# FFN duos with the last up product collected onto a difference in its PSUM bank, the plain up pair at the duo's end, and x reloaded in eight parts

## The chip, the cores and the metric

The kernel runs on one core of a Trainium2 chip. The metric is the device time of the whole program in microseconds, the median of its runs. Times in the profile are microseconds from the start of the profiled execution, unless marked ns. Engines: PE is TensorE, DVE VectorE, ACT ScalarE, POOL GpSimd, SP the engine that issues most DMAs here.

## The reference

A decoder trunk for 256 tokens, d_model 2048, d_ff 5632, all in float32: a layer with gated linear attention (GLA) and an FFN, then shared keys and values, then a layer with differential attention and an FFN. The change is in the two FFNs:

```python
def swiglu(h, w_gate_up, w_down):
    gate, up = jnp.split(h @ w_gate_up, 2, axis=-1)
    return (jax.nn.silu(gate) * up) @ w_down
...
f = swiglu(rmsnorm(x, pre_ffn_g[i]), ffn_w_gate_up[i], ffn_w_down[i])
x = x + rmsnorm(f, post_ffn_g[i])
```

The rows of `rmsnorm` are scaled late: a factor `rs[b]` per token of the 128-token half b (b = 0, 1) is applied to the products.

## The kernel before, in words

**Split products.** Every float32 operand is split into a `hi` and a `lo` part, and each product is three matmuls (`triple`, L482 to 488: hi x hi, hi x lo, lo x hi). A weight sub-tile of 128 x 1024 is loaded by SP into a ring of 5 tiles `raw` (L263), cast to `hi` by ACT (L298) and its rest `lo` = raw - hi made by DVE (L301), in a ring of 9 (NRING). A matmul has 512 columns, so a sub-tile serves two k-blocks (j = 0, 1) of 128 rows, with 512 output columns. The sub-tiles follow one order written by `weight_stream`, the same in which `take` asks for them.

**An FFN.** There are 11 chunks c of 512 gate columns; gate chunk c and up chunk 11 + c make one gated chunk `sg` (silu(gate) x up, 2 halves of 128 tokens). PE transposes it (`split_T`, L655), ACT and DVE split it into `f_ffn_gT` (L657, L658), and the down product (`down_act`, `mm_act`, L411 to 413) uses it. `ffn_steps` mixes up chunks with down steps of earlier groups, FF_GROUPS = ((0, 1), (2, 3), (4, 5), (6, 7), (8,), (9, 10)). Down sums of a group start from the sum so far, copied by ACT into PSUM (L464), and are brought out by ACT (L1261).

**A duo.** Chunk 0 is computed plainly. For c = 1 to 10, `gated_duo` computes gate and up chunk together; I call it duo c. The k dimension has 8 steps s of two k-blocks. At fast steps (s = 0, 2, 3, 4, 5, 6; for c = 1: 0, 2, 4, 6) the 2 x 2 block product (two token halves and two k-blocks by two column chunks) takes 7 products instead of 8, with sums of weights made by DVE (L333, four adds of 512 a step) and sums of h made once (`f_ffn_fast`, `f_ffn_rest`). Each fast step takes four converted sub-steps: "a" (wide, banks 0 and 1), "b" (wide, banks 6 and 2), "c" (wide, banks 5 and 3) and "d" (512 wide, bank 4): 7 x 3 = 21 matmuls. At plain steps (s = 1 and 7; for c = 1: 1, 3, 5, 7) gate goes straight to banks 1 and 3 (token halves 0 and 1) and up to banks 2 and 7, 12 matmuls each. `duo_apart` (the version with bank 7 of its own) runs this in the order of s.

**The end of a duo.** After the last fast step `early` brings out ACT's copy sg0 = bank 0, then on DVE v = bank 5 - sg0, sg1 = bank 6 - v, y = bank 4 - sg1, v = bank 4 + v. After the gate's step 7 `late` adds banks 1 and 3 to sg0 and sg1 and applies Silu. After the up part's step 7 it adds bank 2 to v and bank 7 to y (L1186), and `gated` multiplies each into sg (L1190). `gate_T`, with the transposes, follows some ticks later (`defer`; a tick is one product group). EARLY_BEHIND and LATE_BEHIND hold `early` and `late` behind the conversions of so many of the next sub-steps (`behind`).

**Order.** A framework lays the program out per engine by its own timeline and picks buffers of the pools; each engine then runs its instructions in that order. PSUM has six banks of pool `acc` and two of pool `tp`; in a duo, banks 0 to 5 come from `acc`, 6 and 7 from `tp`. x lies in DRAM meanwhile; at the start of the last down step `reload` (L1463) brings it back in two DMAs of 1 MB for the residual sum at the FFN's end (`after` in FFN 0, then the norm `h_kv` for the next stage, L705).

Of the kernel before, what the change touches and what calls it, by code (L numbers as in the profile page):

```python
# [82 lines left out]
def weight_stream():  # L83

    out = []

    def chunk(name, n, ns=8, s0=0):
        out.extend((name, (n, s0 + s), "plain") for s in range(ns))

    def block(name, n):  # L90
        out.extend((name, (n, s), "plain") for s in range(2))

    def duo(c1, c2, fast):
        for s in range(8):
            if s in fast:
# [24 lines left out]
    def middle_duo(name, fast):  # L120
        chunk(name, 0)
        duo((name, 1), (name, 2), fast)
        chunk(name, 3)

    middle_duo("gla_w_out", FAST_OUT)
    ffn(0)
    chunk("w_v", 0)
    chunk("w_v", 3)
    duo(("w_v", 1), ("w_v", 2), FAST_V)
    for name in ("w_k", "diff_w_q"):  # L130
        for n in range(KT):
            block(name, n)
    middle_duo("diff_w_out", FAST_OUT)
    ffn(1)
    return out

# [52 lines left out]
class Trunk:  # L189
# [289 lines left out]
            for u in range(n, len(order)):  # L479
                run(u, b)  # L480

    def triple(self, ps, a, w, j, first, last):  # L482
        nc = self.nc
        ah, al = a
        wh, wl = (t[:, j * C : (j + 1) * C] for t in w)
        nc.tensor.matmul(ps, ah, wh, start=first, stop=False)  # L486
        nc.tensor.matmul(ps, ah, wl, start=False, stop=False)  # L487
        nc.tensor.matmul(ps, al, wh, start=False, stop=last)  # L488

    def duo_act(self, aT, forms, fast, c1, c2, early, late):  # L490

# [688 lines left out]
    def gated_duo(self, hT, forms, w, c, rs, new_sg):  # L1180

        nc = self.nc
        made = []

        def op(out, in0, in1, how):
            nc.vector.tensor_tensor(out=out, in0=in0, in1=in1, op=how)  # L1186

        def gated(b, up):
            sg = made[0]
            nc.vector.scalar_tensor_tensor(  # L1190
                out=sg[:, b, :], in0=up, scalar=rs[b], in1=sg[:, b, :], op0=ALU.mult, op1=ALU.mult
            )

        def early(ps):
            made.extend((new_sg(), self.scratch(), self.scratch()))
            sg, v, y = made
            nc.scalar.copy(sg[:, 0, :], ps[0])
            op(v, ps[5], sg[:, 0, :], ALU.subtract)
            op(sg[:, 1, :], ps[6], v, ALU.subtract)
            op(y, ps[4], sg[:, 1, :], ALU.subtract)  # L1200
            op(v, ps[4], v, ALU.add)

        def late(bank, ps):
            sg, v, y = made
# [9 lines left out]
        self.duo_apart(hT, forms, ffn_pairs(c), ((w, c), (w, 11 + c)), early, late)  # L1214
        return made[0]

    def ffn(self, fp, hT, rs, gi, wgu, wd, post, after, name, reload, side=None):
# [55 lines left out]
        for n, (kind, which, *chunks) in enumerate(plan):  # L1273
            if kind == "up":
                sg = self.gated_duo(hT, forms, wgu, which, rs, new_sg) if which else gated_first()
                follow = plan[n + 1]
                wait = 4
                if follow[0] == "down" and which not in follow[1]:
                    wait = 2 * len(down_order(*follow[1:])) + 1
                self.defer(wait, lambda sg=sg, c=which: gate_T(sg, c))  # L1280
                continue
            chunks, skew = chunks[0], 0
            if not f:
                f.append(self.whole(5, [P, 2, D], name))
# [168 lines left out]
    def run(self):  # L1453
# [6 lines left out]
        def reload(src, name):  # L1460
            self.x = self.whole(4, [P, 2, D], name)
            for b in range(2):
                nc.sync.dma_start(self.x[:, b, :], src[b])  # L1463

        with tc.tile_pool(name="gla", bufs=1) as gp:
            oT = self.gla(gp, hT, rs)
            rs = []
# [16 lines left out]
        with tc.tile_pool(name="ffn0", bufs=1) as fp:  # L1484
# [9 lines left out]
            self.ffn(fp, hT, rs, 1, "w_gu0", "w_d0", t["post_ffn_g"][0:1], after, "f_ffn0", lambda: reload(x_mix0, "x_ffn0"), self.setup_diff)  # L1494

        hq = Split([None, None])

# [52 lines left out]
        with tc.tile_pool(name="ffn1", bufs=1) as fp:  # L1550

            def store(b, xs):
                for c, xc in enumerate(xs):
                    nc.sync.dma_start(t["out"][b * P : (b + 1) * P, c * C : (c + 1) * C], xc)

            self.ffn(fp, hT, rs, 0, "w_gu1", "w_d1", t["post_ffn_g"][1:2], store, "f_ffn1", lambda: reload(x_mix1, "x_ffn1"))


@with_exitstack
# [89 lines left out]
```

## Time and profile before

| | us |
|---|---|
| three runs | 2168.75, 2168.73, 2167.71; median 2168.73 |
| profiled execution | 2168.14, of which the span from first to last instruction is 2166.4 |
| mean granted clock of TensorE | 0.999 |

The span holds the GLA layer up to about 400 us, FFN 0 to about 1080, values, keys, queries, attention and its output to about 1480, and FFN 1 to the end. In the rows of the profile stand: the start and duration of an instruction (or of a run of equal ones, "x3" with the time of all), its engine, line and operation, out<-in by the program's names, and in square brackets how long the engine had been idle and who released it. A group's row has the line, shapes, count, busy time and the mean of one in ns, then the idle time ahead of them. A window's row has each engine's busy time in that stretch. A row of waits has the total, the number and the longest. In the profile `hs` is a scratch tile (v or y here).

### The profile page before, as it was taken

What the parts mean: (1) busy time and instruction counts of PE and PEld (TensorE: products, weight loads), DVE (VectorE), ACT (ScalarE), POOL (GpSimd) and SP (SyncE); (2) the same over time, 40 slices, a digit from 0 to 9 for tenths busy, and PEclk for the clock granted to TensorE, in tenths of its full rate; (3) what the DMA queues carried; (4) which work ended last, traced back from release to release, by engine and by line L of the source; (5) the groups of instructions that cost most, each with busy time, mean ns of one, the idle gap of its engine ahead of it and who ended that gap; (6) DMA issues with size and microseconds to landing.
All of it is one profiled execution on the core that took longest, in us unless ns stands there. A gap on an engine that the chain in (4) does not pass through costs nothing.

```text
span 2166.4 us, 28415 instructions
## 1 busy us (share of the span) xinstructions
PE 2151.2 (99%) x10044; PEld 1787.7 (83%) x10044; DVE 1953.3 (90%) x2686; ACT 1374.2 (63%) x1926; POOL 37.1 (2%) x66
## 2 busy tenths in 40 slices
PE   9999999999999999999999999999999999999998
PEld 8888788888888888888778888888888888888886
DVE  7989988999999999999798567889999999999996
ACT  8756655666666666666776445556656666666664
POOL 1000000000000000000000000000000000000000
PEclk9999999999999999999999999999999999999999
DMA  8546566666565666656767655465665566665664
GB/s 310 166 150 192 174 226 219 219 199 227 173 209 203 211 211 195 223 190 211 254 200 245 185 179 159 155 226 202 225 195 187 177 207 214 212 209 201 203 225 155
DMA packets 123317, 440.10 MB, mean 203 GB/s; under 512 B 13900, under 2 KB 16629, under 8 KB 121381
## 3 DMA queue, kind: packets, MB, share of 16 engines
q1 hardware_dynamic: 121996, 436.44, 60.4%
q10 hardware_dynamic: 1176, 1.84, 0.2%
q8 instruction: 79, 1.29, 0.2%
q14 instruction: 66, 0.53, 0.1%
HBM read 429.82 MB, written 9.97 MB: 203 GB/s over the span
## 4 chain that ended last, share of the span: by engine, by line
PE 93%; DVE 4%; issue 1%; ACT 1%; DMA 1%; SPq 0%; POOL 0%; DVEq 0%; POOLq 0%; ACTq 0%
PE acc L488 12%; PE acc L487 12%; PE acc L486 12%; PE acc L413 11%; PE acc L412 11%; PE acc L411 11%; PE acc L634 8%; PE acc L635 4%; PE tp L487 2%; PE tp L486 2%; PE tp L488 2%; DVE lo L301 2%; PE tp L655 1%; DVE raw L333 1%; DMA raw<-in_w_d_dram 1%
## 5 line engine op out<-in xcount | busy, mean ns | idle before, releaser
L301 DVE TENSOR_TENSOR lo<-raw,hi 128x1024 fp32r<-128x1024 f32 x921 | 1096.2, 1220 | 115.1 <-ACT hi L298 108.8
L298 ACT CAST hi<-raw 128x1024 fp32r<-128x1024 f32 x923 | 943.9, 1051 | 356.5 <-DVE raw L333 91.5
L412 PE MATMUL acc<-lo,f_ffn_gT 128*128 128x512 f32 x704 | 273.5, 389 | 0.1
L411 PE MATMUL acc<-hi,f_ffn_gT 128*128 128x512 f32 x704 | 270.4, 389 | 0.0
L413 PE MATMUL acc<-hi,f_ffn_gT 128*128 128x512 f32 x704 | 269.0, 389 | 0.0
L487 PE MATMUL acc<-lo,h_ffn 128*128 128x512 f32 x612 | 238.7, 390 | 0.0
L488 PE MATMUL acc<-hi,h_ffn 128*128 128x512 f32 x612 | 238.4, 389 | 0.0
L486 PE MATMUL acc<-hi,h_ffn 128*128 128x512 f32 x612 | 227.8, 390 | 0.0
L333 DVE TENSOR_TENSOR raw<-raw 128x512 f32<-128x512 f32 x232 | 159.5, 687 | 3.4
L411 PEld LDWEIGHTS acc<-hi,f_ffn_gT 128*128 128x128 f32 x704 | 132.2, 188 | 28.4 <-issue 0.6
L412 PEld LDWEIGHTS acc<-lo,f_ffn_gT 128*128 128x128 f32 x704 | 132.1, 188 | 27.9 <-DVE lo L301 0.6
L413 PEld LDWEIGHTS acc<-hi,f_ffn_gT 128*128 128x128 f32 x704 | 132.2, 188 | 27.4
L486 PEld LDWEIGHTS acc<-hi,h_ffn 128*128 128x128 f32 x612 | 114.9, 188 | 24.2 <-ACT hi L298 0.4
L488 PEld LDWEIGHTS acc<-hi,h_ffn 128*128 128x128 f32 x612 | 114.9, 188 | 23.5
L487 PEld LDWEIGHTS acc<-lo,h_ffn 128*128 128x128 f32 x612 | 114.9, 188 | 23.5
L298 ACT CAST hi<-sum 128x512 fp32r<-128x512 f32 x72 | 44.8, 622 | 101.1 <-DVE sum L333 101.1
L634 PE MATMUL acc<-h_q,hi 128*128 128x512 f32 x256 | 92.5, 401 | 0.0
L634 PE MATMUL acc<-h_kv,hi 128*128 128x512 f32 x256 | 90.7, 399 | 0.0
L634 PE MATMUL acc<-h_mix,hi 128*128 128x512 f32 x256 | 90.6, 398 | 0.0
L1261 ACT COPY f_ffn<-acc 128x512 f32<-128x512 f32 x80 | 45.8, 586 | 66.4 <-PE acc L413 66.4
L298 ACT CAST f_ffn_rest<-sum 128x512 fp32r<-128x512 f32 x56 | 34.9, 623 | 80.9 <-DVE sum L333 80.9
L333 DVE TENSOR_TENSOR sum<-raw,raw 128x512 f32<-128x512 f32 x116 | 79.4, 685 | 0.0
(415 smaller groups left out, 4128.6 us busy)
## 6 DMA issues: line engine op xcount, KB each, us to landing
raw<-in_w_gu_dram SPq DMA_DIRECT2D x352, 512.0 KB, 4.5
raw<-in_w_d_dram SPq DMA_DIRECT2D x176, 512.0 KB, 4.8
raw<-in_gla_w_r_dram SPq DMA_DIRECT2D x32, 512.0 KB, 4.8
raw<-in_gla_w_v_dram SPq DMA_DIRECT2D x32, 512.0 KB, 4.1
raw<-in_gla_w_out_dram SPq DMA_DIRECT2D x32, 512.0 KB, 4.5
raw<-in_w_v_dram SPq DMA_DIRECT2D x32, 512.0 KB, 4.4
raw<-in_w_k_dram SPq DMA_DIRECT2D x32, 512.0 KB, 4.4
raw<-in_diff_w_q_dram SPq DMA_DIRECT2D x32, 512.0 KB, 3.5
```

Of the source, the lines that this page charges most:

```text
L298: cast = nc.scalar.copy(hi, src)
L301: rest = eng.tensor_tensor(out=lo, in0=src, in1=hi.bitcast(F32), op=ALU.subtract)
L333: return self.nc.vector.tensor_tensor(out=out, in0=in0, in1=in1, op=ALU.add)
L411: nc.tensor.matmul(ps, ah, rh, start=(kt == 0 and not onto), stop=False, skip_group_check=onto)
L412: nc.tensor.matmul(ps, ah, rl, start=False, stop=False, skip_group_check=onto)
L413: nc.tensor.matmul(ps, al, rh, start=False, stop=(kt == 2 * ns - 1), skip_group_check=onto)
L486: nc.tensor.matmul(ps, ah, wh, start=first, stop=False)
L487: nc.tensor.matmul(ps, ah, wl, start=False, stop=False)
L488: nc.tensor.matmul(ps, al, wh, start=False, stop=last)
L634: nc.tensor.matmul(ps, lh, aT.both(kt), start=(kt == 0), stop=False)
L635: nc.tensor.matmul(ps[:, SEQ:], ll, aT.hi(kt), start=False, stop=(kt == KT - 1))
L1261: nc.scalar.copy(fc, ps)
```

## The change

`duo_seeded` takes the place of `duo_apart` in the FFNs (proj_out and values keep `duo_apart`).

- At the plain steps ahead of the last fast step only the gate's sub-tile stays. The up sub-tile of such a step ("kept") moves behind the last fast step, ahead of the gate's step 7; `weight_stream` is changed alike. Its bank 2 part runs at once, its bank 7 part after the gate's step 7.
- `early` has no y: it writes bank 4 - sg1 straight into PSUM bank 7, which is opened after the last fast step. The matmuls of bank 7 then all accumulate onto it (no `start`), and `late` gives bank 7 to `gated` as it is. One DVE add per duo is gone.
- Bank 7 now comes from `acc`, and banks 2 and 6 from `tp`.
- `early` is `urgent` (high priority), EARLY_BEHIND goes from 3 to 1, and chunk 0's `gate_T` waits 1 tick and not 4.
- x is reloaded as 8 DMAs of 256 KB, deferred by 4 + 3n ticks.

```diff
-EARLY_BEHIND, LATE_BEHIND, DOWN_BEHIND, GATE_BEHIND = 3, 3, 0, 0
+RELOAD_BEGIN, RELOAD_EVERY = 4, 3
+EARLY_BEHIND, LATE_BEHIND, DOWN_BEHIND, GATE_BEHIND = 1, 3, 0, 0
...
+    def duo_seeded(self, aT, forms, fast, chunks, early, late):
...
+        def bank_of(bank):
+            if bank not in ps:
+                ps[bank] = self.tp().rearrange("p j t -> p (j t)") if bank in (2, 6) else self.acc()
+                return True
+            return False
+
+        def add(bank, a, wp, j, last, onto=False):
+            first = bank_of(bank)
+            self.triple(ps[bank], a, wp, j, first and not onto, last, onto)
...
+            if s not in fast:
+                wp = self.take(w1, (n1, s))
+                for b, bank in enumerate((1, 3)):
+                    plain(bank, s, b, wp, False)
+                self.free()
+                held.append(s)
+                continue
...
+            if last:
+                bank_of(7)
+                with self.behind(EARLY_BEHIND):
+                    self.urgent(early)(ps)
+        kept = [(s, self.take(w2, (n2, s))) for s in held]
+        for s, wp in kept:
+            plain(2, s, 0, wp, False)
+        wp = self.take(w1, (n1, 7))
+        for b, bank in enumerate((1, 3)):
+            plain(bank, 7, b, wp, True)
+        for s, wp2 in kept:
+            plain(7, s, 1, wp2, False, True)
+            self.free()
+        self.free()
+        wp = self.take(w2, (n2, 7))
+        plain(2, 7, 0, wp, True)
+        plain(7, 7, 1, wp, True, True)
+        self.free()
...
         def early(ps):
-            made.extend((new_sg(), self.scratch(), self.scratch()))
-            sg, v, y = made
+            made.extend((new_sg(), self.scratch()))
+            sg, v = made
...
-            op(y, ps[4], sg[:, 1, :], ALU.subtract)
+            op(ps[7], ps[4], sg[:, 1, :], ALU.subtract)
...
+            elif bank == 2:
+                op(v, ps[bank], v, ALU.add)
+                gated(0, v)
             else:
-                b, part = (0, v) if bank == 2 else (1, y)
-                op(part, ps[bank], part, ALU.add)
-                gated(b, part)
+                gated(1, ps[bank])
...
-                wait = 4
+                wait = 4 if which else 1
...
+        def reload_by_parts(src, name):
+            self.x = x = self.whole(4, [P, 2, D], name)
+            for n in range(8):
+                b, c = n // 4, slice(n % 4 * C, (n % 4 + 1) * C)
+                self.defer(RELOAD_BEGIN + RELOAD_EVERY * n, lambda b=b, c=c: nc.sync.dma_start(x[:, b, c], src[b][:, c]))
```

The order of instructions at three places follows; a number behind a name tells tiles of one kind apart.

ACT at the start of duo 5 of FFN 0, before. `f_ffn0_4438<-acc` are the evacuations of the down step that ran ahead of it, the `hi` are wide casts of weights, and `f_ffn0_rest<-sum` is the narrow cast of a fast step's sub-step "d" (which uses spare room in that tile):

```order
L298 CAST hi_1168_6112<-raw_1144_5988 128x1024
L298 CAST hi_1171_6146<-raw_1150_6012 128x1024
L298 CAST hi_1176_6168<-raw_1153_6021 128x1024
L298 CAST hi_1179_6186<-raw_1159_6049 128x1024
L1261 COPY f_ffn0_4438<-acc_1174_6152 128x512
L1261 COPY f_ffn0_4438<-acc_1175_6153 128x512
L298 CAST f_ffn0_rest_3649<-sum_1181_6202 128x512
L657 CAST f_ffn0_gT4_6243<-tp_1190_6244 128x4x128
L298 CAST hi_1182_6207<-raw_1167_6098 128x1024
```

The same place after:

```order
L306 CAST hi_1164_6104<-raw_1140_5975 128x1024
L306 CAST hi_1167_6138<-raw_1146_5996 128x1024
L306 CAST hi_1172_6160<-raw_1152_6038 128x1024
L306 CAST f_ffn0_rest_3649<-sum_1174_6176 128x512
L306 CAST hi_1175_6181<-raw_1155_6044 128x1024
L1335 COPY f_ffn0_4436<-acc_1170_6144 128x512
L1335 COPY f_ffn0_4436<-acc_1171_6145 128x512
L306 CAST hi_1178_6199<-raw_1152_6038 128x1024
L306 CAST hi_1183_6229<-raw_1163_6090 128x1024
```

The narrow cast of the first fast step, and the wide cast next to it, stood behind the two evacuations and now stand ahead of them.

DVE at the end of duo 10 of FFN 0, before: `acc` and `tp` are PSUM banks, `hs` scratch, `raw_1795` the first down weight, and `sg` the gated chunk:

```order
L301 TENSOR_TENSOR lo_1816_9184<-raw_1795_9098,hi_1815_9183 128x1024
L1186 TENSOR_TENSOR hs_1837_9256<-acc_1767_8967,sg_1836_9255 128x512
L301 TENSOR_TENSOR lo_1819_9196<-raw_1803_9132,hi_1818_9195 128x1024
L1186 TENSOR_TENSOR sg_1836_9255<-tp_1763_8955,hs_1837_9256 128x512
L1186 TENSOR_TENSOR sg_1836_9255<-acc_1758_8932,sg_1836_9255 128x512
L301 TENSOR_TENSOR lo_1822_9205<-raw_1806_9144,hi_1821_9204 128x1024
L1186 TENSOR_TENSOR hs_1838_9257<-acc_1773_8986,sg_1836_9255 128x512
L1186 TENSOR_TENSOR hs_1837_9256<-acc_1773_8986,hs_1837_9256 128x512
L301 TENSOR_TENSOR lo_1825_9217<-raw_1811_9163,hi_1824_9216 128x1024
L301 TENSOR_TENSOR lo_1828_9229<-raw_1814_9175,hi_1827_9228 128x1024
L1186 TENSOR_TENSOR sg_1836_9255<-acc_1768_8971,sg_1836_9255 128x512
L1186 TENSOR_TENSOR hs_1838_9257<-tp_1777_9016,hs_1838_9257 128x512
```

The same place after, where `raw_1790` is the first down weight and `acc_1823` is bank 7:

```order
L1259 TENSOR_TENSOR hs_1825_9220<-acc_1759_8954,sg_1824_9219 128x512
L309 TENSOR_TENSOR lo_1800_9135<-raw_1779_9049,hi_1799_9134 128x1024
L1259 TENSOR_TENSOR sg_1824_9219<-tp_1753_8935,hs_1825_9220 128x512
L309 TENSOR_TENSOR lo_1803_9147<-raw_1782_9061,hi_1802_9146 128x1024
L309 TENSOR_TENSOR lo_1806_9159<-raw_1790_9095,hi_1805_9158 128x1024
L1259 TENSOR_TENSOR acc_1823_9218<-acc_1764_8968,sg_1824_9219 128x512
L1259 TENSOR_TENSOR hs_1825_9220<-acc_1764_8968,hs_1825_9220 128x512
L309 TENSOR_TENSOR lo_1809_9168<-raw_1793_9107,hi_1808_9167 128x1024
L1259 TENSOR_TENSOR sg_1824_9219<-acc_1748_8912,sg_1824_9219 128x512
L1259 TENSOR_TENSOR sg_1824_9219<-acc_1760_8958,sg_1824_9219 128x512
L309 TENSOR_TENSOR lo_1812_9180<-raw_1798_9126,hi_1811_9179 128x1024
L1259 TENSOR_TENSOR hs_1825_9220<-tp_1754_8939,hs_1825_9220 128x512
```

The difference goes into `acc_1823`; the add of the earlier bank 7 (`tp_1777`) into scratch, the last row before, is gone, and the adds of banks 1 and 3 stand next to each other. The first `lo` of a down weight stands ahead of the difference.

SP around the reload of FFN 0, before; `w_gu0` are gate and up weights of duo 10, `w_d0` down weights:

```order
L263 DMA raw_1783_9042<-in_w_gu0_dram 128x1024
L263 DMA raw_1786_9054<-in_w_gu0_dram 128x1024
L1463 DMA x_ffn0_9307<-x_mix0_2816 128x2048 x2
L263 DMA raw_1792_9086<-in_w_gu0_dram 128x1024
L263 DMA raw_1795_9098<-in_w_d0_dram 128x1024
L263 DMA raw_1803_9132<-in_w_d0_dram 128x1024
```

And after:

```order
L271 DMA raw_1773_9017<-in_w_gu0_dram 128x1024
L1543 DMA x_ffn0_9287<-x_mix0_2816 128x512 x3
L271 DMA raw_1779_9049<-in_w_gu0_dram 128x1024
L1543 DMA x_ffn0_9287<-x_mix0_2816 128x512 x2
L271 DMA raw_1782_9061<-in_w_gu0_dram 128x1024
L1543 DMA x_ffn0_9287<-x_mix0_2816 128x512 x3
L271 DMA raw_1790_9095<-in_w_d0_dram 128x1024
L271 DMA raw_1793_9107<-in_w_d0_dram 128x1024
```

The eight parts stand in three clumps between the last two `w_gu0` loads and the first `w_d0` load; of the 2 MB none has moved behind a `w_d0` load.

More of the change, by code (lines that the diff above doesn't have):

```diff
@@ L93, in duo @@
     def duo(c1, c2, fast):
+        apart = c1[0][:4] == "w_gu"
+        kept = [s for s in range(7) if s not in fast] if apart else []
         for s in range(8):
+            if s == 7:
+                out.extend((c2[0], (c2[1], s), "plain") for s in kept)
+            if s in kept:
+                out.append((c1[0], (c1[1], s), "plain"))
+                continue
             if s in fast:
@@ L480, in down_act, with plain @@
                 run(u, b)
-    def triple(self, ps, a, w, j, first, last):
+    def duo_seeded(self, aT, forms, fast, chunks, early, late):
+        ps, held = {}, []
+        (w1, n1), (w2, n2) = chunks
+        def bank_of(bank):
[6 more added lines that the diff above has]
+            self.triple(ps[bank], a, wp, j, first and not onto, last, onto)
+        def plain(bank, s, b, wp, last, onto=False):
+            for j in range(2):
+                add(bank, aT.tokens(2 * s + j, b), wp, j, last and j == 1, onto)
+            if last:
+                with self.behind(LATE_BEHIND):
+                    late(bank, ps)
+            self.tick()
+        for s in range(7):
+            k1, k2 = 2 * s, 2 * s + 1
+            if s not in fast:
[4 more added lines that the diff above has]
+                held.append(s)
+                continue
+            f, last = forms.pairs.index(s), s == fast[-1]
+            plan = {
+                "a": ((0, aT.tokens(k1, 0)), (1, aT.tokens(k2, 0))),
+                "b": ((6, forms.fast(f, 2)), (2, forms.fast(f, 3))),
+                "c": ((5, forms.fast(f, 1)), (3, aT.tokens(k2, 1))),
+                "d": ((4, forms.fast(f, 0)),),
+            }
+            for kind, prods in plan.items():
+                wp = self.take("duo", (*chunks, s), kind)
+                for j, (bank, a) in enumerate(prods):
+                    add(bank, a, wp, j, last and bank in (0, 4, 5, 6))
+                self.free()
+                if kind != "d":
+                    self.tick()
+            if last:
+                bank_of(7)
[14 more added lines that the diff above has]
+        plain(7, 7, 1, wp, True, True)
+        self.free()
@@ L483, in triple @@
+    def triple(self, ps, a, w, j, first, last, onto=False):
         nc = self.nc
@@ L485, in triple @@
         wh, wl = (t[:, j * C : (j + 1) * C] for t in w)
-        nc.tensor.matmul(ps, ah, wh, start=first, stop=False)
-        nc.tensor.matmul(ps, ah, wl, start=False, stop=False)
-        nc.tensor.matmul(ps, al, wh, start=False, stop=last)
+        nc.tensor.matmul(ps, ah, wh, start=first, stop=False, skip_group_check=onto)
+        nc.tensor.matmul(ps, ah, wl, start=False, stop=False, skip_group_check=onto)
+        nc.tensor.matmul(ps, al, wh, start=False, stop=last, skip_group_check=onto)
     def duo_act(self, aT, forms, fast, c1, c2, early, late):
@@ L1199, in early @@
             op(sg[:, 1, :], ps[6], v, ALU.subtract)
[L1200 removed]
+            op(ps[7], ps[4], sg[:, 1, :], ALU.subtract)
             op(v, ps[4], v, ALU.add)
         def late(bank, ps):
[L1204 removed]
+            sg, v = made
             if bank in (1, 3):
@@ L1208, in late @@
                 nc.scalar.activation(sg[:, b, :], sg[:, b, :], AF.Silu, scale=rs[b])
-            else:
-                b, part = (0, v) if bank == 2 else (1, y)
-                op(part, ps[bank], part, ALU.add)
-                gated(b, part)
-        self.duo_apart(hT, forms, ffn_pairs(c), ((w, c), (w, 11 + c)), early, late)
+            elif bank == 2:
+                op(v, ps[bank], v, ALU.add)
+                gated(0, v)
+            else:
+                gated(1, ps[bank])
+        self.duo_seeded(hT, forms, ffn_pairs(c), ((w, c), (w, 11 + c)), early, late)
         return made[0]
@@ L1492, in after @@
                 self.defer(4, lambda: nc.sync.dma_start(x_dram[b], self.x[:, b, :]))
-            self.ffn(fp, hT, rs, 1, "w_gu0", "w_d0", t["post_ffn_g"][0:1], after, "f_ffn0", lambda: reload(x_mix0, "x_ffn0"), self.setup_diff)
+            self.ffn(fp, hT, rs, 1, "w_gu0", "w_d0", t["post_ffn_g"][0:1], after, "f_ffn0", lambda: reload_by_parts(x_mix0, "x_ffn0"), self.setup_diff)
         hq = Split([None, None])
@@ L1554, in store @@
                     nc.sync.dma_start(t["out"][b * P : (b + 1) * P, c * C : (c + 1) * C], xc)
-            self.ffn(fp, hT, rs, 0, "w_gu1", "w_d1", t["post_ffn_g"][1:2], store, "f_ffn1", lambda: reload(x_mix1, "x_ffn1"))
+            self.ffn(fp, hT, rs, 0, "w_gu1", "w_d1", t["post_ffn_g"][1:2], store, "f_ffn1", lambda: reload_by_parts(x_mix1, "x_ffn1"))
 @with_exitstack
```

## The prediction

> **What bounds the kernel now.** I read the page's share of busy time first, then the chain that ended last, the windows of a stretch in the middle of FFN 0, and what TensorE (PE) waits for.
>
> ```profile
> PE 2151.2 (99%) x10044; PEld 1787.7 (83%) x10044; DVE 1953.3 (90%) x2686; ACT 1374.2 (63%) x1926; POOL 37.1 (2%) x66
> PE 93%; DVE 4%; issue 1%; ACT 1%; DMA 1%; SPq 0%; POOL 0%; DVEq 0%; POOLq 0%; ACTq 0%
> 685.00:809.00 124.00, 124.00 (x557) 102.82 (x555) 120.90 (x145) 81.26 (x98) 0.00 (x0) 1.00 0.60 204
> 1079.00:1097.00 18.00, 16.17 (x81) 12.66 (x80) 15.63 (x36) 15.67 (x48) 1.10 (x2) 1.00 0.76 245
> PE tp L655 <- DVE sg L1190: 1.3, 2, 1.0
> ```
>
> In the window 685 to 809 (length, then busy time of PE, PE's weight loads, DVE, ACT, POOL) PE is busy for all of 124.00 us, and DVE for 120.90, 97%. PE sets the time, and DVE could set it with little more work. The last row says what PE loses inside the FFNs: twice, 1.3 us together, it waits with the transposes (L655) of a gated chunk for DVE's product `gated` (L1190). On PE that place is:
>
> ```profile
> 1044.44 0.39 PE L413 MATMUL acc<-hi,f_ffn_gT 128*128 128x512 f32 x1
> 1044.67 0.61 PE L411 MATMUL acc<-hi,f_ffn_gT 128*128 128x512 f32 x2
> 1046.30 0.55 PE L655 MATMUL tp<-ident,sg 128*128 128x128 f32 x3 [1.01 <-DVE sg L1190]
> 2124.06 0.98 PE L655 MATMUL tp<-ident,sg 128*128 128x128 f32 x7 [0.31 <-DVE sg L1190]
> ```
>
> Matmuls follow each other every 0.227 us (1044.44 to 1044.67). After 1044.67 two are due, at 1044.67 and 1044.89, and the transposes would start at about 1045.1: the loss is 1.2 us in FFN 0 (the bracket's 1.01, counted from a matmul's end, and a start-up), and by the same rule 0.5 us in FFN 1 (bracket 0.31). Both are in duo 10, the last. At the join of FFN 0 and the next stage (1079 to 1097) PE lacks another 1.83 us of 18.00. So in the stretches that the change touches the most to be won is 1.2 + 0.5 + 1.8 = 3.5 us; the rest of PE's gaps lies ahead of FFN 0, where the program stays as it is. Against that stands everything that could make DVE late.
>
> **The matmuls and the add that goes.** The order has as many matmuls after as before, so 10,044 times 0.227 us stays. DVE loses one 512-wide add in each of 20 duos (10 in each FFN).
>
> ```profile
> L301 DVE TENSOR_TENSOR lo<-raw,hi 128x1024 fp32r<-128x1024 f32 x60 | 71.0, 1220 | 0.5
> L333 DVE TENSOR_TENSOR sum<-raw,raw 128x512 f32<-128x512 f32 x12 | 8.2, 685 | 0.0
> L1190 DVE SCALAR_TENSOR_TENSOR sg<-hs,rs_ffn,sg 128x512 f32<-128x512 f32 x4 | 2.8, 746 | 0.0
> L1186 DVE TENSOR_TENSOR hs<-acc,hs 128x512 f32<-128x512 f32 x4 | 2.7, 681 | 0.0
> L464 ACT COPY acc<-f_ffn 128x512 f32<-128x512 f32 x8 | 4.6, 579 | 0.0
> 1017.76 3.64 DVE L301 TENSOR_TENSOR lo<-raw,hi 128x1024 fp32r<-128x1024 f32 x3
> 1024.46 3.64 DVE L301 TENSOR_TENSOR lo<-raw,hi 128x1024 fp32r<-128x1024 f32 x3
> ```
>
> The add is the L1186 row, 0.68 us, 0.60 when it follows another at once. 20 x 0.60 = 12 us less on DVE; off PE's path it is worth nothing by itself. The remaining subtraction now writes into PSUM (bank 7). No row shows DVE writing to PSUM. ACT's write into PSUM (L464) took 0.58, DVE's dearest 512-wide operation (L1190) 0.75; I take the subtraction's own 0.68 from the L1186 row, which is nearest, and keep -0.10 to +0.07 us per duo, which is DVE time with cover.
>
> The last product now reads bank 7 where it read SBUF. DVE's rows show no surcharge for that: 681 ns with a PSUM operand (L1186), 685 without (L333). The Trainium skill, in "VectorE: DVE Perf Modes", section on the TRN2 errata, has a source in PSUM dearer by 62 cycles at 0.96 GHz, which would be an estimated 65 ns on each of 20 products, 1.3 us of DVE; the trace does not bear it out.
>
> **The up pair moved to the duo's end.** This is the term I worry about. The pair of step 1 (12 matmuls, 12 x 0.227 = 2.72 us) leaves the place ahead of fast steps 2 to 6, so PE reaches each of these 2.72 us earlier, and DVE has one `lo` fewer ahead of them (spacing 1.16 us: 3.64 for three, less the last one's tail). Left alone that costs 2.72 - 1.16 = 1.56 us of DVE's lead over PE. In a fast step DVE needs 6.70 us (1017.76 to 1024.46, above) and PE 21 x 0.227 = 4.77, so the lead shrinks over the run of steps and is least at step 6. There it is:
>
> ```profile
> 714.17 3.90 ACT L298 CAST hi<-raw 128x1024 fp32r<-128x1024 f32 x4 [0.70 <-PE acc L488]
> 715.57 0.39 PE L486 MATMUL acc<-hi,f_ffn_rest 128*128 128x512 f32 x1
> 775.32 3.90 ACT L298 CAST hi<-raw 128x1024 fp32r<-128x1024 f32 x4 [0.70 <-DVE raw L333]
> 777.66 0.39 PE L486 MATMUL acc<-hi,f_ffn_rest 128*128 128x512 f32 x1
> L298 ACT CAST hi<-raw 128x1024 fp32r<-128x1024 f32 x60 | 60.9, 1051 | 14.5 <-DVE raw L333 9.9 <-DMA raw<-in_w_d_dram 2.9 <-DMA raw<-in_w_gu_dram 1.2
> ```
>
> The first cast of each ACT row ends 1.05 us after its start (1051 ns) and frees the third sub-step's first matmul: 715.22 against 715.57 leaves 0.35 us in duo 5; 776.37 against 777.66 leaves 1.29 us in duo 6. The duos come in these two kinds: as little as duo 5's in duos 5, 7, 9 and 10 of both FFNs (8 places), 1.0 to 1.3 in seven others. A loss of 1.56 would make PE stall at all 15.
>
> What gives the lead back is the duo's start. Duo 5 begins so:
>
> ```profile
> 681.84 0.59 ACT L1261 COPY f_ffn<-acc 128x512 f32<-128x512 f32 x1 [2.72 <-PE acc L413]
> 683.20 0.59 ACT L1261 COPY f_ffn<-acc 128x512 f32<-128x512 f32 x1 [0.77 <-PE acc L413]
> 683.68 0.62 ACT L298 CAST f_ffn_rest<-sum 128x512 fp32r<-128x512 f32 x1
> 684.33 0.69 DVE L301 TENSOR_TENSOR f_ffn_rest<-sum,f_ffn_rest 128x512 fp32r<-128x512 f32 x1 [1.48 <-ACT f_ffn_rest L298]
> 988.43 4.63 DVE L301 TENSOR_TENSOR lo<-raw,hi 128x1024 fp32r<-128x1024 f32 x4 [0.70 <-ACT hi L298]
> 996.02 0.69 DVE L658 TENSOR_TENSOR f_ffn_gT<-tp,f_ffn_gT 128x512 fp32r<-128x512 f32 x1 [0.43 <-ACT f_ffn_gT L657]
> ```
>
> ACT holds a narrow cast behind two evacuations that wait for PE, and DVE stands idle for 1.48 us. In the new order this cast, and a wide one, come ahead of the two copies. So DVE saves 1.16 + 1.48 = 2.64 against PE's 2.72: the lead falls from 0.35 to 0.27, no stall. In duo 10 it saves 1.16 + 0.70 + 0.43 (the last two rows' idle time) + 0.60 (duo 9's add) = 2.89 against 2.72, about as before. I take 0.3 us for both FFNs, for the scatter at eight places with some 0.2 us left each. From both sides: -0.1 (a stall can't be less than none, and PE shows next to none now) and 8 x (1.56 - 0.35) + 7 x (1.56 - 1.29) = 11.6 us.
>
> **The seed and the late rows.** From the `lo` that precedes it to the seed's end DVE does, at spacing, v 0.60, lo 1.16, `sg` 0.60, two lo 2.32, seed 0.60: 5.3 us. Bank 7's first matmul on PE stands 35 matmuls behind that `lo`'s first use, 7.9 us: the seed has 2.6 us to spare, so it makes no wait. In duo 10 the second `gated` needs bank 7's last matmul, and from there PE has 28 matmuls, 6.4 us, until the transposes; two products at 0.67 need 1.4. DVE's rows up to them (before: 3.49 + 1.41 us, below) end earlier by an add and by the head start, so the waits of 1.2 and 0.5 us go, though the transposes stand 8 matmuls earlier.
>
> ```profile
> 1041.43 3.49 DVE L301 TENSOR_TENSOR lo<-raw,hi 128x1024 fp32r<-128x1024 f32 x3
> 1044.83 1.41 DVE L1190 SCALAR_TENSOR_TENSOR sg<-hs,rs_ffn,sg 128x512 f32<-128x512 f32 x2
> ```
>
> If they stay, the transposes' earlier place makes them no longer than 8 x 0.227 = 1.8 us more each.
>
> **The reload in eight parts.** The order shows that they aren't spread: 3, 2 and 3 of them stand between the last loads of the duo, and all stand ahead of the first `w_d` load, as the two big ones did. Same 2 MB, same place in the queue, 6 issues more in each FFN.
>
> ```profile
> x_ffn<-x_mix SPq DMA_DIRECT2D x4, 1024.0 KB, 5.8
> gain<-in_post_ffn_g_dram SPq DMA_DIRECT2D x8, 256.0 KB, 4.5
> 1018.97 0.80 SPq L1463 DMA_DIRECT2D x_ffn<-x_mix  x2
> 1019.87 0.38 SPq L263 DMA_DIRECT2D raw<-in_w_gu_dram  x1
> 1028.88 1.06 ACT L298 CAST hi<-raw 128x1024 fp32r<-128x1024 f32 x1 [0.25 <-DMA raw<-in_w_d_dram]
> 1031.61 1.05 ACT L298 CAST hi<-raw 128x1024 fp32r<-128x1024 f32 x1 [1.20 <-DMA raw<-in_w_d_dram]
> 1025.70 5.83 DMA raw<-in_w_d_dram
> SPq L263 <- DVE lo L301: 20.7, 9, 5.0
> SPq L1463 <- PE acc L488: 5.0, 1, 5.0
> ```
>
> Six issues at 0.40 (0.80 for two) are 2.4 us of SP. They are hidden as long as SP waits anyway: in 1000 to 1030 it waits 20.7 us for raw buffers (next to last row) and 5.0 for PE to free x's room (last row). Without that cover: up to 2.4 per FFN, 4.8. The first `w_d` load now takes its buffer from the last fast step, as the second did before: that `lo` ended at 1025.60, the load was issued at 1025.70 and took 5.83 us. DVE being 2.6 us earlier, I put the issue at 1023.1 and the landing at 1027.9 to 1028.9. PE wants this tile 17 matmuls after the point of least lead, in duo 10 at 1026.03 (row of the same kind as 715.57, with 0.35 us of lead), so at 1029.9; minus a cast of 1.05, landing is due by 1028.8. That is no slack: I charge 0.3 us per FFN, 0.6; bounds 0 and 2.4 each.
>
> **The rest.** EARLY_BEHIND and the shorter wait for chunk 0's transposes move rows that have microseconds of room; nothing. The join at 1079: its transposes stand 34 matmuls behind the earlier rows' last matmul before and after, so its 1.8 us stay (bounds -1.8 and +0.5).
>
> **The sum.** Profiled execution 2168.14 - 1.2 - 0.5 (gate waits) + 0.3 (lead) + 0.6 (first `w_d`) = 2167.3. The median of the three runs lies 0.6 above the profiled execution, so 2167.9: no change. A measurement of this kernel can tell about 0.2%, 4.3 us, from no change; same is 2164.4 to 2173.1.
>
> **Rivals.** First, the lead is drained: the head start does not come, since the early casts find no raw tile or no place in the ring, and PE stalls on ACT's cast at step 6. It decides once more than 0.35 us of the 1.56 isn't regained. Price in full 11.6 instead of 0.3: 2167.9 + 11.3 = 2179.2, slower. For it: 97% on DVE and 0.35 us at eight places. Against: the idle 1.48 us is seen, and the order takes its cause away. Chance 0.13.
>
> Second, the parts wait for each other, each taking its 4.5 us (the 256 KB row) in turn: 8 x 4.5 = 36.0 against 2 x 5.8 = 11.6, so `w_d` lands up to 24 us later in each FFN, 2167.9 + 49 = 2217 at worst, and it decides from the first microsecond. Against: two transfers of 1 MB and two loads, 3 MB, were through in the 9.9 us from 1018.97 to the cast at 1028.88, so transfers overlap. Chance 0.03. The Trainium skill, in "DMA: Bandwidth & Descriptors", section "Anatomy of one DMA", has about 2.0 us fixed and bytes over 436 GB/s for each DMA, fitted on DMAs that GpSimd issues; in turn that would be an estimated 8 x 2.6 = 20.8 against 2 x 4.4 = 8.8, 12 us later. The overlap in the trace speaks against adding them up.
>
> Third, the change doesn't do what it says: the parts are one clump (as the order has it), and the gate waits stay because `gated` still stands behind the `lo` of the down weights: 2168.14 + 0.3 + 0.6 + 0.6 = 2169.6, no change. Chance 0.18.
>
> Fourth, the join's 1.8 us goes too, through x's earlier landing or an earlier DVE: 2167.9 - 1.8 - 0.9 (no new stalls) = 2165.2, still no change; only something unforeseen beside it gives faster. Chance 0.10.
>
> The forecast itself has 0.56. Faster by over 0.2%: 0.05, out of the fourth. Slower: 0.13 + 0.03, and 0.02 for the issue cover gone with a part of the first, 0.18. Same: 0.77. The range starts at the fourth rival, with half a microsecond below it, 2164.5; above it takes the third rival, the issue bound (2167.9 + 4.8) and the first rival's beginning, to 2175. Left out is most of the first and the second rival.
>
> **What would show it.** Right: the wait of L655 for `gated` gone from PE's waits in both FFNs; 20 fewer adds on DVE; DVE's 1.48 us idle at odd duos' start gone; at step 6 casts ending 0.1 to 0.4 us ahead of their matmul; the DVE write to PSUM at 0.6 to 0.75 us; the first `w_d` landing within half a microsecond of need. Wrong: rows of PE waiting for `hi` of ACT at step 6 of several duos, or PE waiting for the seed or for the `w_d` DMA by over 2 us, or DVE's busy time not down by some 12 us.

## The result, and the profile after

The changed kernel takes 2177.03 us (median of 6 runs, 2176.25 to 2179.26) where the kernel before takes 2167.61 (6 runs): the ratio is 1.0043, with a 95% interval of 1.003 to 1.0056. It is slower by some 9 us. The profiled execution's span is 2174.5 us against 2166.4. The prediction, 2167.9 and no change, was wrong, and its range ended below the result.

The page after, with the row of busy times and the chain that ended last, and the first row of what PE waits for:

```profile
PE 2153.9 (99%) x10044; PEld 1785.0 (82%) x10044; DVE 1942.6 (89%) x2666; ACT 1376.5 (63%) x1926; POOL 38.4 (2%) x66
PE 88%; DVE 5%; DMA 3%; ACT 2%; issue 1%; SPq 0%; POOL 0%; ACTq 0%; DVEq 0%; POOLq 0%
PE acc L419 <- ACT acc L472: 6.0, 9, 1.4
```

DVE has 20 instructions and 10.7 us less to do, as it should. PE waits no more for `gated`: no row of the transposes (now L728) for L1263 is left among its waits. In its place stands a row that before had no counterpart: the first matmul of a down step (L419) waits for ACT's copy of the sum so far into PSUM (L472), nine times, 6.0 us. The chain of waits has DMA at 3% where it had 1%. Here is one such place, at the end of duo 5 of FFN 0, on PE and on ACT, and the load in the chain:

```profile
719.28 0.39 PE L561 MATMUL acc<-hi,h_ffn 128*128 128x512 f32 x1
719.99 0.50 PE L419 MATMUL acc<-hi,f_ffn_gT 128*128 128x512 f32 x1 [0.33 <-ACT acc L472]
```

```profile
716.27 1.05 ACT L306 CAST hi<-raw 128x1024 fp32r<-128x1024 f32 x1 [0.37 <-DMA raw<-in_w_d_dram]
718.39 1.06 ACT L306 CAST hi<-raw 128x1024 fp32r<-128x1024 f32 x1 [1.07 <-DMA raw<-in_w_d_dram]
719.35 1.10 ACT L472 COPY acc<-f_ffn 128x512 f32<-128x512 f32 x2
```

```profile
713.85 4.46 DMA raw<-in_w_d_dram
1026.43 6.94 DMA raw<-in_w_d_dram
```

Matmuls follow each other every 0.227 us, so PE should have issued the down matmul at 719.51 and did so at 719.99; the matmul behind it came 0.34 us later, not 0.23, so the place cost 0.6 us. The copies that it needs could not start before 719.35, because ACT runs in order and the cast ahead of them waited 1.07 us for a load issued at 713.85. That cast is of the second down weight, which the first down matmul doesn't need at all. In the kernel before, the first copy stands behind the second down weight's cast too. The two copies end at 720.36 and 722.51, later than after (some 719.9 and 720.45), and hurt nobody, for PE issues the first down matmul at 723.27 only:

```profile
718.83 1.05 ACT L298 CAST hi<-raw 128x1024 fp32r<-128x1024 f32 x1 [0.27 <-DMA raw<-in_w_d_dram]
719.78 0.58 ACT L464 COPY acc<-f_ffn 128x512 f32<-128x512 f32 x1
720.97 1.05 ACT L298 CAST hi<-raw 128x1024 fp32r<-128x1024 f32 x1 [0.61 <-DMA raw<-in_w_d_dram]
721.93 0.58 ACT L464 COPY acc<-f_ffn 128x512 f32<-128x512 f32 x1
723.27 0.39 PE L411 MATMUL acc<-hi,f_ffn_gT 128*128 128x512 f32 x1
```

So it is PE that has changed. The order of ACT after shows what it now runs into (`hi_1239` and `hi_1242` are the first two down weights, `hi_1236` is the up part's step 7):

```order
L306 CAST hi_1236_6459<-raw_1220_6378 128x1024
L306 CAST hi_1239_6471<-raw_1226_6410 128x1024
L306 CAST hi_1242_6480<-raw_1229_6422 128x1024
L472 COPY acc_1268_6598<-f_ffn0_4436 128x512
L472 COPY acc_1269_6599<-f_ffn0_4436 128x512
L306 CAST hi_1245_6492<-raw_1232_6439 128x1024
```

On PE the first matmul on `acc_1268` is number 3277 in the order; before, the first of that down step was number 3294. It stands 17 places earlier: 14 down matmuls have gone ahead of bank 7's twelve, and the first of them also ahead of five of bank 2's. It is the same in duos 3 to 10 of both FFNs (in duo 2 the first down matmul moved by 2 places in FFN 0 and by 7 in FFN 1). I take it that the framework did this because the seed (the difference in bank 7, on which its matmuls wait) is planned late on DVE; no run tests the framework's reason. PE asks 17 x 0.227 = 3.9 us earlier for a copy that ACT has 0.4 us earlier.

Over the FFNs, what the larger gaps between the starts of two matmuls (over 0.26 us) have beyond 0.227 us was added up: in FFN 0 some 6.8 us after against 3.2 before, in FFN 1 6.7 against 1.9. That is 8.4 us more, the gate waits' saving already taken off; the span is 8.1 us longer.

### The profile page after: what moved, and what is told of

It reads as the page before. It is cut to its first block, busy times and chain, and to the rows that moved or that the text cites. A ratio compares the mean times of both kernels' runs of the same rounds, so it can differ in the third digit from the quotient of the medians.

```text
span 2174.5 us, 28418 instructions
## 1 busy us (share of the span) xinstructions
PE 2153.9 (99%) x10044; PEld 1785.0 (82%) x10044; DVE 1942.6 (89%) x2666; ACT 1376.5 (63%) x1926; POOL 38.4 (2%) x66
## 4 chain that ended last, share of the span: by engine, by line
PE 88%; DVE 5%; DMA 3%; ACT 2%; issue 1%; SPq 0%; POOL 0%; ACTq 0%; DVEq 0%; POOLq 0%
PE acc L419 11%; PE acc L421 11%; PE acc L420 11%; PE acc L560 10%; PE acc L561 10%; PE acc L559 10%; PE acc L707 8%; PE acc L708 4%; PE tp L561 3%; PE tp L560 3%; PE tp L559 3%; DMA raw<-in_w_d_dram 2%; DVE lo L309 2%; ACT hi L306 2%; DVE raw L341 1%
## 5 line engine op out<-in xcount | busy, mean ns | idle before, releaser
L419 PE MATMUL acc<-hi,f_ffn_gT 128*128 128x512 f32 x704 | 270.5, 392 | 6.1 <-ACT acc L472 6.0
L419 PEld LDWEIGHTS acc<-hi,f_ffn_gT 128*128 128x128 f32 x704 | 132.1, 188 | 38.6 <-ACT acc L472 11.1
```

Of the source, the lines that this page charges most:

```text
L419: nc.tensor.matmul(ps, ah, rh, start=(kt == 0 and not onto), stop=False, skip_group_check=onto)
```

## The experiments

My first theory, as the expectations have it: the down weights come too late for PE's new order. The rivals: the conversions' lead is drained (the first rival of the prediction), and the reload in parts holds up the down loads. Each run is compared with the kernel before on its own chip.

**x in two DMAs again**, the rest as changed (the same edit in FFN 1).

```diff
-... lambda: reload_by_parts(x_mix0, "x_ffn0"), self.setup_diff)
+... lambda: reload(x_mix0, "x_ffn0"), self.setup_diff)
```

> The changed kernel with x reloaded in two DMAs of 1 MB as before. Theory 1 (late down weights: the up tile that was moved stands between the last fast step and the down weights, so the first down loads take their raw buffers later, while PE's order asks for them 17 matmuls earlier; PE waits behind ACT's copy of the sum so far, which stands behind a down weight's cast): the stalls of duos 2 to 9 stay, only those of duo 10 can shrink, 2174 to 2177. Theory 2 (conversion lead over the fast steps drained): unchanged, 2177. Theory 3 (the eight parts hold the down loads up): nearly all comes back, 2168 to 2170.

Measured: 2176.34 us against 2168.27, ratio 1.0043 (1.0028 to 1.0058). The parts aren't the main cause. The waits for the copy stayed. (The profiled execution is the longest of the four, 2181.85 us, with two stretches of 3.41 us at half the clock, so its waits are somewhat larger than those of the other three.)

```profile
PE acc L419 <- ACT acc L472: 7.5, 10, 1.8
```

**The move alone.** The kernel before, with the up pair of the early plain steps moved behind the last fast step; no seed.

```diff
+            if moved and s == 7:
+                for u in kept:
+                    wp = self.take(chunks[1][0], (chunks[1][1], u))
+                    for b, bank in enumerate((2, 7)):
+                        for j in range(2):
+                            add(bank, aT.tokens(2 * u + j, b), wp, j, False)
...
+                    if banks == (2, 7) and s in kept:
+                        continue
```

> The kernel before with only the up pair of the early plain steps moved behind the last fast step; bank 7 accumulates from zero in its own bank, the add stays, x comes in two DMAs. Its first down matmul stands where it stood before (17 matmuls later than in the changed kernel). Theory 1: the loads are late as in the changed kernel, but PE asks 3.9 us later, so most stalls go, 2168 to 2172. Theory 2: the lead is lost just as much, 2176 to 2178. Theory 3: no parts, so 2168.

Measured: 2166.92 against 2168.27, ratio 0.9994 (0.9984 to 1.0003). Moving the pair costs nothing that can be measured; the gate waits went here too. PE waits for a cast at step 6 in two places, 0.2 and 0.3 us, so the lead over the fast steps is nearly all kept, and a late load alone does no harm: in duo 5 the second down weight's cast starts at 718.65, no earlier than in the changed kernel (718.39). That is the second theory refuted; what remains must come with the seed, with what the framework made of it, or with the banks' pools and the places of `early` and `gate_T`, which changed too.

**The gate's step 7 moved up** into the place that the up pair left, so that two tiles and not three stand between the last fast step and the down weights.

```diff
+                if s == kept[-1]:
+                    out.append((c1[0], (c1[1], 7), "plain"))
```

> The changed kernel with the gate's step 7 put into the place that the up pair left (behind the gate's first plain step; for duo 1 behind the third), so that two tiles and not three stand between the last fast step and the down weights, and banks 1 and 3 are done with the last fast step. Theory 1: down loads as early as before, the first down matmul 5 matmuls later than in the changed kernel, 2167 to 2171. Theory 2: the lead at step 6 as before, 2167 to 2169. Theory 3: duo 10 as in the changed kernel, the rest gone by neither reason, 2176.

Measured: 2224.97 against 2168.27, ratio 1.0261 (1.0244 to 1.0278), far from all three theories. The row of waits and ACT's order at the end of duo 5 (`hi_1242` to `hi_1251` are the second to the fifth down weight; the first, `hi_1239`, is cast ahead of these rows):

```profile
PE acc L422 <- ACT acc L475: 39.8, 16, 4.0
```

```order
L1273 COPY sg_1261_6550<-acc_1184_6225 128x512
L309 CAST hi_1242_6489<-raw_1229_6428 128x1024
L309 CAST hi_1245_6498<-raw_1232_6440 128x1024
L309 CAST hi_1248_6510<-raw_1235_6457 128x1024
L309 CAST hi_1251_6522<-raw_1238_6469 128x1024
L475 COPY acc_1268_6598<-f_ffn0_4436 128x512
```

The casts of five down weights stand ahead of the copies instead of two; in this place three of them wait for their own load and the fifth for PE. PE's wait went from some 0.7 us to 2.5 on average. Part of the 57 us isn't in these waits: PE also ran at half its clock after some of them (last section). The run that missed all theories showed the piece that I had left out: the place of the copies on ACT.

**The down step held behind bank 7**, the changed kernel otherwise:

```diff
+            with self.past(self.seven if onto else None):
+                nc.tensor.matmul(ps, ah, rh, start=(kt == 0 and not onto), stop=False, skip_group_check=onto)
```

> The changed kernel, seed, parts and all, with the first matmul of a down step that starts from a copied sum held in order behind the duo's last matmul of bank 7. So PE's first down matmul stands where it stood before. Theory 1, now sharper (the seed makes PE's order put the first 17 down matmuls ahead of bank 7's matmuls; ACT's copies of the sum so far stand behind the second down weight's cast, which waits for its load; late loads alone do no harm, as the run with the move only showed): the waits of L419 for the copy go, 2166 to 2168. If the seed itself is what comes late, PE waits for it instead, in many duos: 2172 or more.

Measured: 2171.15 against 2167.93, ratio 1.0014 (1.0005 to 1.0023). The waits for the copy are gone, and 6 of the 9 us with them (9.4 over the kernel before without the hold, 3.2 with it). What is left is in duo 10: PE waits for the seed (L1263), 2.1 and 1.5 us, for DVE has the `lo` of the first down weight ahead of the seed, and that load is late.

```profile
PE acc L561 <- DVE acc L1263: 3.3, 2, 1.9
```

**The parts alone**, put into the kernel before:

> The kernel before with x in eight parts and nothing else. Theory 1: nothing or a little in duo 10, 2167.5 to 2169. Theory 3 (parts hold up the down loads) has fallen as the main cause; as a small one it gives 2169 to 2171 by waits for down weights in duo 10 of each FFN.

Measured: 2171.76 against 2167.93, ratio 1.0017 (1.0008 to 1.0026), 3.8 us slower. SP, ACT and PE's waits in duo 10 of FFN 0:

```profile
1019.83 1.75 SPq L1470 DMA_DIRECT2D x_ffn<-x_mix  x4
1021.68 0.38 SPq L264 DMA_DIRECT2D raw<-in_w_gu_dram  x1
1022.10 0.94 SPq L1470 DMA_DIRECT2D x_ffn<-x_mix  x2
1023.14 0.40 SPq L264 DMA_DIRECT2D raw<-in_w_d_dram  x1
1023.58 1.14 SPq L1470 DMA_DIRECT2D x_ffn<-x_mix  x2
```

```profile
1026.54 7.71 DMA raw<-in_w_d_dram
1034.33 1.05 ACT L299 CAST hi<-raw 128x1024 fp32r<-128x1024 f32 x1 [2.24 <-DMA raw<-in_w_d_dram]
PE tp L656 <- DVE sg L1191: 2.9, 2, 1.5
PE acc L412 <- ACT acc L465: 1.9, 2, 1.2
```

The two large DMAs were issued within 0.80 us; the eight small ones, with the loads between them, take from 1019.83 to 1024.72. The second down load, issued at 1026.54, then needs 7.71 us where the same one took 5.83 before. So the parts have a cost of their own, in duo 10 alone, which the changed kernel's other waits partly hide.

**A sixth raw buffer**, with 8 places in the ring in place of 9, in the changed kernel. (Beside 9 places a sixth buffer has no room: the GLA layer's pool takes 14.03 KB per partition and 12.5 are left. So that variant has no time.)

> The changed kernel with 6 raw buffers and 8 places in the ring of hi and lo (for room). Down loads can start one buffer earlier, casts one place later. Theory 1: the second down weight's cast no longer waits about 1 us for its load, so the waits for ACT's copy shrink in duos 3 to 9, 2169 to 2173, unless the shorter ring makes the casts late. If the loads have no part in it, 2177 or more.

Measured: 2177.78 against 2167.93, ratio 1.0044 (1.003 to 1.0058). The waits for the copy did shrink, from nine to three (3.3 us), but others came, for `hi` in four places and at the join after FFN 0. It fits that the loads have a part in the waits, and settles nothing else, for two things were changed at once.

**Down matmuls ahead, without a seed.** The move alone, with bank 7's last 12 matmuls held behind the first 12 of the down step:

```diff
+                                with self.past(self.lead):
+                                    for j in range(2):
+                                        add(7, aT.tokens(2 * u + j, 1), up, j, u == 7 and j == 1)
```

> The kernel with the move only (no seed, add kept, x in two DMAs), but with bank 7's 12 matmuls of the two late up tiles put behind the first 12 down matmuls. Theory 1: the seed isn't needed for the loss, only the order is: waits of the first down matmul for ACT's copy come back, 2170 to 2178 (the copy of the second half can stand behind the second cast, the first one not). If the seed's own write to PSUM, or its wait, is the cause: 2167, as with the move only.

Measured: 2168.38 against 2167.93, ratio 1.0002 (0.9993 to 1.0011). The expectation of 2170 or more was wrong: here the framework put one copy ahead of the second cast and one behind it, and PE waits 0.3 us in all for a copy. So down matmuls ahead of bank 7's cost little by themselves; but the first of them stands 12 places earlier here, not 17 as in the changed kernel.

**The same with the copies behind the second cast:**

```diff
+                    second = self.parts[self.n_take + 1][0] if u == 0 else None
+                    with self.past(second):
+                        for i in range(2):
+                            self.nc.scalar.copy(ps[c][i], base(c, i))
```

> The unseeded kernel whose first 12 down matmuls stand ahead of bank 7's, now with ACT's two copies of the sum so far held behind the cast of the second down weight, as they stand in the changed kernel. Theory 1: it is this place in ACT's order that makes PE wait, so the waits of the first down matmul come in most duos without any seed, 2171 to 2176. If the place on ACT doesn't matter: 2168.4, as the run without it.

Measured: 2175.89 against 2168.67, ratio 1.0034 (1.0021 to 1.0048). The time is what theory 1 gives, but the waits are mostly others:

```profile
PE acc L420 <- ACT f_ffn_gT L697: 3.9, 6, 0.9
PE acc L420 <- ACT acc L475: 1.1, 2, 0.6
```

The edit also moved the transposed chunk's cast (L697) in the duos where it comes ahead of a down step. And the copies themselves hardly delay PE, which asks 12 places earlier, not 17: in duo 5 they are done at 720.79, and the first down matmul starts at 721.12. So the run is no proof, and for the copies it is a miss: it says only that PE is as sensitive to ACT's order at the other cast.

**The copies ahead of the second cast**, in the changed kernel, with its seed, its parts, and its order on PE up to bank 7's last matmul in each duo:

```diff
+    def second(self, n):
+        down = [u >= 0 and self.stream[u][0][:3] == "w_d" for u in (n - 2, n - 1, n)]
+        return down == [False, True, True]
...
+            if self.second(self.n_conv) and self.n_take < self.n_conv:
+                break
...
-        cast = nc.scalar.copy(hi, src)
+        with self.past(self.copied if self.second(self.n_conv) else None):
+            cast = nc.scalar.copy(hi, src)
```

> The changed kernel, with its order on PE, its seed and its eight parts, but with the cast of the second down weight held behind ACT's copies of the sum so far. Theory 1: the waits in duos 2 to 9 go (about 0.6 us each, some 6 us in all), duo 10 still waits for its loads, 2170 to 2173. If the place on ACT doesn't matter: 2177.

Measured: 2169.90 against 2168.67, ratio 1.0007 (0.9997 to 1.0016). ACT at the end of duo 5, and what is left of the waits:

```profile
716.81 1.05 ACT L307 CAST hi<-raw 128x1024 fp32r<-128x1024 f32 x1 [0.23 <-DMA raw<-in_w_d_dram]
717.77 1.10 ACT L479 COPY acc<-f_ffn 128x512 f32<-128x512 f32 x2
719.02 1.06 ACT L307 CAST hi<-raw 128x1024 fp32r<-128x1024 f32 x1 [0.15 <-DMA raw<-in_w_d_dram]
```

```profile
PE acc L426 <- ACT acc L479: 2.3, 2, 1.2
```

The copies now start at 717.77 and not at 719.35. Of nine waits two are left, in duo 10, and 8 of the 9 us are gone (9.4 over the kernel before without this edit, 1.2 with it), though the first 14 down matmuls are as early on PE as in the changed kernel. Holding the down step back on PE had taken away the same waits. So it takes both, PE's early request and the copies' place on ACT, and this settles the main cause.

**The same with x in two DMAs:**

> As the run before, with x in two DMAs of 1 MB: what is left of the parts' cost goes too, 2167 to 2169 by theory 1; if the parts cost nothing beside the order (as they seemed to when they alone were taken out of the changed kernel, 0.7 us), as the run before.

Measured: 2168.61 against 2168.67, ratio 1.0000 (0.9991 to 1.0009).

**The down step held and x in two DMAs:**

> The changed kernel with the down step's first matmul held behind bank 7's last one, as in the run before, and with x in two DMAs of 1 MB. Theory 1 (PE's order with ACT's copy, and apart from it the eight parts in duo 10): both costs are gone, 2166 to 2168, level with the kernel before or 1 us under it. If the seed's place on DVE is itself a cause, PE still waits for it in duo 10, 2169 to 2171.

Measured: 2169.18 against 2168.67, ratio 1.0006 (0.9997 to 1.0015). Neither the seed's waits nor the copy's are left. About 1.2 us remain at one place, a wait for `hi` in duo 10 of FFN 1, where a weight's load stands behind x (the run before has it too).

So each of two repairs (the down step held, the copies ahead) takes the changed kernel back to the kernel before once the parts are out. Both keep the seed, the banks' new pools and the new places of `early` and `gate_T`, so these cost nothing that can be measured. None beats the kernel before by more than the measurement can tell; the move alone, 1.35 us under it, comes nearest.

## Why the prediction was wrong, point by point

- **What bounds the kernel: right.** PE bound, with DVE close; at most a few us to win. Even the best variant was only 1.35 us under the kernel before, which its interval doesn't tell from nothing.
- **The add that goes: right.** 20 instructions and 10.7 us of DVE (12 forecast), worth nothing by itself: with both costs repaired and the add gone the time is 2168.61 against 2168.67. The DVE write to PSUM takes what the other additions take:

```profile
L1259 DVE TENSOR_TENSOR acc<-acc,sg 128x512 f32<-128x512 f32 x2 | 1.4, 691 | 0.0
L1259 DVE TENSOR_TENSOR sg<-acc,sg 128x512 f32<-128x512 f32 x4 | 2.7, 680 | 0.0
```

- **The lead over the fast steps: right, and with it the first rival's mechanism wrong.** In duo 5 the first cast of this ACT row ends at 712.56, and the matmul that needs it starts at 712.90: 0.34 us of lead, 0.27 forecast, 0.35 before. DVE's 1.48 us of idle time at the duo's start are gone as forecast, though 1.12 us behind a cast came a little later.

```profile
711.51 2.00 ACT L306 CAST hi<-raw 128x1024 fp32r<-128x1024 f32 x2 [0.70 <-PE acc L561]
712.90 0.39 PE L559 MATMUL acc<-hi,f_ffn_rest 128*128 128x512 f32 x1
```

  The rival's time of 2179.2 lies near the result, but by another cause: the run with the move only has the same pair moved, waits 0.5 us in all at step 6, and is not slower. That the time of this rival came near is luck.
- **"So it makes no wait" of the seed: the step that failed.** The working counted 35 matmuls between the seed's `lo` and bank 7's first matmul and took them for cover. To the letter it held: in the changed kernel no row of PE's waits is for the seed. But the working did not ask what those matmuls were. Fourteen of them are the next down step's, which had stood behind bank 7. Their overlap was taken as given; in duos 3 to 10 they brought the need for the down weights and for ACT's copies 17 places, 3.9 us, forward, which the sum has at nothing outside duo 10. The runs showed nine waits for the copy in its place, 6.0 us, and 8 of the 9 us went with the copies' place on ACT. I had the copies' row (L464) before me, and used it only for the price of a PSUM write.
- **"I charge 0.3 us per FFN" for the first down weight: the same step, mis-sized where it was made.** It did count from the earlier need, but for duo 10 only, and for the tile's own cast. The landing was put at 1027.9 to 1028.9. In the changed kernel the load was issued at 1026.43 (the chain's row above); less the 3.1 us that the waits in duos 5 to 9 had already cost that is 1023.3, against 1023.1 forecast. But it took 6.94 us, not up to 5.83 (7.71 behind the small DMAs in the run with the parts alone), and landed at 1033.37. In duo 10 the copies stand right behind the first down weight's cast, so here it is that load itself that PE waits for, by way of ACT: 1.6 us, and 1.2 us at the same place in FFN 1, against 0.3 each:

```profile
1033.44 1.04 ACT L306 CAST hi<-raw 128x1024 fp32r<-128x1024 f32 x1 [2.98 <-DMA raw<-in_w_d_dram]
1033.20 0.39 PE L561 MATMUL acc<-hi,h_ffn 128*128 128x512 f32 x1
1035.03 0.50 PE L419 MATMUL acc<-hi,f_ffn_gT 128*128 128x512 f32 x1 [1.44 <-ACT acc L472]
```

- **The parts: the upper bound was nearer than the value.** "They are hidden as long as SP waits anyway" held in part. In the run with the parts alone the rows of DVE are 0.84 us later than before (1025.30 against 1024.46); on this scale the first down load was issued 1.95 us later (1023.14 against 1020.35), as SP's wait lies ahead of the parts. The second was issued no later (1026.54 against 1025.70), but took 1.88 us longer, a cost that the issues don't have in them. 3.8 us measured in the kernel before, where 0 was taken and 4.8 was the bound. The second rival, each part waiting for the one before, is refuted: it asked for up to 49 us. The Trainium skill, in "DMA: Bandwidth & Descriptors", section "Anatomy of one DMA", has 2.0 us for each DMA, fitted on DMAs that GpSimd issues; added up, that would have made the parts land an estimated 12 us later. The load behind them took 1.88 us longer than before (7.71 against 5.83), so the trace doesn't agree with adding them up.
- **The gate waits: right.** They went, in the changed kernel and with the move alone. The third rival, that they stay, is refuted.
- **The join: right.** In the rows of PE's waits it has 1.0 us for `h_kv` and 0.7 for `x_T` after, 1.5 and 0.3 before. The fourth rival, that this goes too, is refuted.

## What to carry to other kernels

When a change lets an engine run something earlier, ask for everything that this something needs, on every engine, and not only whether the thing that moved is ready: here the down step needed a weight, and a copy that stood in ACT's order behind a cast of another weight that was still being loaded. Cover counted in matmuls is only cover if these matmuls have their own operands in time; look at what they are in the order. And a small instruction that feeds the busiest engine should not stand behind one that waits for a DMA which it doesn't need.

## What the runs showed of the hardware

In the run with the gate's step 7 moved up, PE ran at half its clock after some of its waits. Here are matmuls on either side of a wait of 3.96 us, and windows of 5 us ahead of it, just behind it and a little later (the number behind the five engines is the granted clock):

```profile
921.97 0.39 PE L564 MATMUL tp<-hi,h_ffn 128*128 128x512 f32 x1
926.31 0.80 PE L422 MATMUL acc<-hi,f_ffn_gT 128*128 128x512 f32 x1 [3.96 <-ACT acc L475]
926.90 0.63 PE L423 MATMUL acc<-lo,f_ffn_gT 128*128 128x512 f32 x1
927.33 0.63 PE L424 MATMUL acc<-hi,f_ffn_gT 128*128 128x512 f32 x1
```

```profile
915.00:920.00 5.00, 5.00 (x24) 4.14 (x23) 4.94 (x6) 4.76 (x6) 0.00 (x0) 1.00 0.59 211
926.30:931.30 5.00, 4.99 (x12) 3.97 (x13) 5.00 (x7) 4.68 (x7) 0.00 (x0) 0.50 0.91 316
932.00:937.00 5.00, 5.00 (x24) 4.12 (x23) 1.50 (x2) 1.22 (x2) 0.00 (x0) 1.00 0.36 129
```

The spacing is 0.43 us instead of 0.23, the clock 0.50, and 5 us pass with 12 matmuls instead of some 22 (5 / 0.227): in these 5 us alone the wait cost another 2.3 us. It is not the length of the wait alone that decides. In the same run the wait of 3.07 us below kept the clock, and the one of 2.00 us lost it, a few matmuls later:

```profile
667.10 0.50 PE L422 MATMUL acc<-hi,f_ffn_gT 128*128 128x512 f32 x1 [3.07 <-ACT acc L475]
1057.10 0.50 PE L422 MATMUL acc<-hi,f_ffn_gT 128*128 128x512 f32 x1 [2.00 <-ACT acc L475]
661.98:665.39 3.41, 2.05 (x10) 1.35 (x8) 3.37 (x4) 2.08 (x2) 0.00 (x0) 1.00 1.00 388
665.39:668.81 3.42, 1.71 (x7) 1.42 (x8) 3.42 (x5) 3.30 (x5) 0.00 (x0) 1.00 0.92 338
668.81:672.22 3.41, 3.41 (x17) 2.81 (x15) 3.41 (x5) 2.98 (x5) 0.00 (x0) 1.00 0.87 305
1054.51:1057.92 3.41, 1.41 (x7) 0.85 (x6) 2.62 (x4) 3.17 (x5) 0.00 (x0) 1.00 1.07 407
1057.92:1061.33 3.41, 3.41 (x10) 2.63 (x9) 3.41 (x5) 3.41 (x6) 0.00 (x0) 0.50 0.89 270
```

The windows are cut where the clock changed, and at whole multiples of 3.413 us from there. In the clock records of this run the halved stretches start at 600.54, 924.80, 1057.92, 1703.04, 1771.31, 1901.02, 2034.14, 2102.40 and, past the last matmuls, 2218.45; they lie whole multiples of 3.413 us apart (1057.92 is 600.54 + 134 x 3.413), and all but the last take 3.41 or 6.83 us. Cut on this grid, each one follows a stretch of 3.41 us in which PE was idle for 1.86 us or more (here 3.41 - 1.41 = 2.00). None follows a stretch with 1.77 us or less: the wait of 3.07 us fell across two, 1.36 and 1.71 us. In the profile of the run with x in two DMAs, 1.77 and 1.78 us were enough. So on these traces the border lies near 1.8 us, about half of a stretch; as the ends of matmuls are modelled, it is no sharper than that.

The Trainium skill, in "TensorE: Matmul & The Clock Gate", Part 1 on the clock gate, has a free-running window of about 3.4 us, and the clock falls after an idle one. That the window runs freely fits the grid, and the 3.07 us that did no harm; that 2.00 us were enough does not fit a window that must be idle throughout.
